# Two attention mixers in a decoder trunk: attention steps at set places between the products, weights split four pieces ahead, rotary on GpSimd

## The chip, the cores and the metric

The kernel runs on one NeuronCore of a Trainium2 chip. The metric is the device time of one launch in microseconds (us). Its engines are named as the profile names them: PE (TensorE matmul), PEld (TensorE weight load), DVE (VectorE), ACT (ScalarE), POOL (GpSimd), SP (SyncE, which issues the DMAs here).

## What is computed

The reference is a two-layer decoder trunk on 256 tokens of width 1024, all in float32. Each layer is a SwiGLU half-step, an attention mixer with 16 heads of 64, and a second SwiGLU half-step (inner width 2816). Cut to what matters here:

```python
def mixer_a(h, w_qkv, w_o, pos):
    qkv = (h @ w_qkv).reshape(B, S, 3, N_HEADS, HEAD_DIM).transpose(2, 0, 3, 1, 4)
    q, k, v = partial_rotary(qkv[0], pos), partial_rotary(qkv[1], pos), qkv[2]
    ...
    return o.transpose(0, 2, 1, 3).reshape(B, S, ATTN_DIM) @ w_o

def mixer_b(h, w_q, w_o, k_pad, v_pad, k_mean, pos):
    q = partial_rotary((h @ w_q)..., pos)
    ...
    return out @ w_o

for layer in range(2):
    h = h + 0.5 * swiglu(rmsnorm(h, ffn1_norm[layer]), ...)
    hn = rmsnorm(h, mix_norm[layer])
    h = h + (mixer_a(hn, ...) if layer == 0 else mixer_b(hn, ...))
    h = h + 0.5 * swiglu(rmsnorm(h, ffn2_norm[layer]), ...)
    if layer == 0:
        shared = shared_kv(h, kv_norm, kv_w, pos)
return rmsnorm(h, final_norm)
```

Mixer a mixes three dilated causal patterns; with 256 tokens they come down to one softmax with a mask that counts in how many patterns a key occurs. Mixer b takes k and v from `shared_kv` and, with one block of 256, is plain causal attention. So both mixers are the same program with other inputs: projections of q, k and v, rotary on 16 of the 64 columns of q and k, masked softmax, values, and an output projection.

## The kernel before

**Exact products.** A float32 operand is split into a high part (rounded by ScalarE, L151 for weights, L89 for others) and the rest (a subtraction on VectorE, L152, L91, L93), and each product is three matmuls: high by high, high by low, low by high (`product`, L177). A piece of weights is 128 partitions by 1024 values; a unit is one raw buffer of 1 MB, mostly two pieces (`unit`, L137; `pieces_of`, L144). There are four raw buffers and eight buffers each for high and low parts.

**The mixer** (`mixer`, L533) works through four groups of four heads. For one group `projections` (L552) forms k and v together, 512 columns wide, 8 blocks of the inner dimension by 2 halves of the tokens, then q, 256 wide; each product is one step of a generator, which yields its estimated cost. ScalarE takes the sums out with the norm's scale (L567, L582), `rotate` (L446) turns 16 columns of each head in four VectorE instructions (L453 to L456), and `turn_in` (L542) transposes q and k on TensorE (L549) and splits them.

**Attention** (`attend`, L458) goes by pairs of heads, eight pairs in all. `scores` (L466): 12 small matmuls (L473) into two PSUM tiles, mask and row minimum on VectorE (L481), exponentials on ScalarE (L484), reciprocal (L486), and the normalisation by four GpSimd instructions (L489). `turn` (L491): three transposes of one head's probabilities (L494) and their split. `values` (L499): four matmuls a head (L508, L510) into one PSUM tile for both heads, brought together by ScalarE and VectorE (L511, L512), and split into a block for the output projection. `out_t` (L409) multiplies the eight blocks; five of them as they come, the last three at the end, one output tile after the other.

**What sets the order.** `weave` (L274) runs two generators side by side, the attention and the feed (projections of the later groups, then output projection), and takes the next step from the one that is behind by its share of the estimated cost (20.4 against 59.0). `START` = 50 steps of the feed go first. A group's attention may begin when `finished` (L585) has marked the group ready. The kernel is written in a framework whose planner then sets each engine's order and the waits: the order of the text counts as priority, and an instruction that the planner takes to be ready may go ahead of an earlier one that it takes to be waiting. On the chip each engine goes through its own list in order.

PSUM is eight banks: five accumulators and three tiles for scores and transposes (`accp`, `trp`).

## Time and profile before

| | us |
|---|---|
| median of 3 runs (lowest, highest) | 1023.26 (1021.39, 1024.11) |
| the profiled execution | 1023.26 |
| its span, first to last instruction | 1021.5 |
| busy: PE / DVE / ACT / POOL | 994.7 / 724.6 / 592.0 / 178.1 |
| mean granted TensorE clock | 0.993 |

The span is what the trace covers; the execution's own time lies 1.8 us above it. Busy time is the time in which an engine had an instruction running. Since matmuls are pipelined and their ends are modelled, a matmul's own duration overlaps the next one's; the distance between starts is what a product costs in a stream. A row of waits names the instruction that stood waiting, what ended the wait, the total, the number of times and the longest. The granted clock is the share of full speed that TensorE was given.

### The profile page before, as it was taken

The page shows a single profiled execution, that of the slowest core. Times are in us where ns is not written, and L with a number is a line of the kernel's source. Part 1 is how long each engine was busy: PE and PEld are TensorE (multiplying, and loading weights), DVE is VectorE, ACT ScalarE, POOL GpSimd, SP SyncE. Part 2 cuts the span into 40 slices and gives each one's busy share as a digit, 9 for nine tenths or more (in the row PEclk, how much of TensorE's full clock was granted, in tenths as well). Part 3 has the DMA queues.
Part 4 walks back from the last instruction along what each step waited for, and adds up shares of the span by engine and source line. Part 5 has one row for each costly group of instructions (what it writes and reads, how often), then busy time and mean ns, then how long its engine had stood idle before and what let it go on. Part 6 is the DMA issues. An engine that isn't in the chain of part 4 may idle for free.

```text
span 1021.5 us, 15730 instructions
## 1 busy us (share of the span) xinstructions
PE 994.7 (97%) x5899; PEld 871.0 (85%) x5899; DVE 724.6 (71%) x1252; ACT 592.0 (58%) x1092; POOL 178.1 (17%) x211
## 2 busy tenths in 40 slices
PE   8999999999899999999999999999999999999997
PEld 6888888887798888888888888888878888888886
DVE  7978865666676788876678878665667678878642
ACT  6766564456666566565456665444666565665531
POOL 3111101203224211110112111010222222111000
PEclk9999999999999999999999999999999999999999
DMA  9885556653331565666655664666333444655611
GB/s 306 254 261 166 195 190 201 198 174 115 124 125 61 184 209 170 191 196 187 206 164 178 198 201 148 224 206 202 129 124 104 144 124 141 207 189 180 207 67 42
DMA packets 158428, 176.05 MB, mean 172 GB/s; under 512 B 3600, under 2 KB 152336, under 8 KB 158352
## 3 DMA queue, kind: packets, MB, share of 16 engines
q1 hardware_dynamic: 157920, 174.50, 53.6%
q8 instruction: 46, 0.75, 0.3%
q10 hardware_dynamic: 432, 0.55, 0.2%
q14 instruction: 30, 0.25, 0.1%
HBM read 173.99 MB, written 1.05 MB: 171 GB/s over the span
## 4 chain that ended last, share of the span: by engine, by line
PE 88%; ACT 6%; DVE 3%; POOL 1%; issue 1%; DMA 0%; POOLq 0%; ACTq 0%; DVEq 0%
PE f_u L191 16%; PE f_g L191 15%; PE dn_f L191 12%; PE f_u L194 8%; PE f_g L194 8%; PE dn_f L194 6%; PE dn_f_d L182 2%; PE dn_f_d L180 2%; PE dn_f_d L184 2%; PE kv_b L184 1%; PE kv_b L182 1%; PE kv_b L180 1%; PE kv_a L184 1%; PE kv_a L180 1%; PE kv_a L182 1%
## 5 line engine op out<-in xcount | busy, mean ns | idle before, releaser
L191 PE MATMUL f_g<-x_n,wh_f_g 128*128 128x512 f32 x688 | 180.1, 394 | 0.0
L191 PE MATMUL f_u<-x_n,wh_f_u 128*128 128x512 f32 x688 | 177.7, 391 | 2.3 <-DVE j_f_g L309 2.3
L191 PEld LDWEIGHTS f_u<-x_n,wh_f_u 128*128 128x128 f32 x688 | 128.8, 188 | 30.2 <-issue 2.1
L191 PEld LDWEIGHTS f_g<-x_n,wh_f_g 128*128 128x128 f32 x688 | 124.0, 189 | 22.6
L327 POOL TENSOR_TENSOR j_f_u<-j_f_u,r_n 128x256 f32<-128x256 f32 x88 | 76.0, 865 | 383.0 <-DVE j_f_u L309 363.8
L191 PE MATMUL dn_f<-act_f,wh_f 128*128 128x512 f32 x528 | 126.5, 391 | 0.0
L152 DVE TENSOR_TENSOR wl_f_u<-raw_f_u,wh_f_u 128x1024 fp32r<-128x1024 f32 x86 | 119.6, 1392 | 1.8 <-ACT wh_f_u L151 1.7
L152 DVE TENSOR_TENSOR wl_f_g<-raw_f_g,wh_f_g 128x1024 fp32r<-128x1024 f32 x86 | 104.5, 1244 | 22.6 <-PE f_g L194 14.4
L191 PEld LDWEIGHTS dn_f<-act_f,wh_f 128*128 128x128 f32 x528 | 96.8, 188 | 18.6
L152 DVE TENSOR_TENSOR wl_f<-raw_f,wh_f 128x1024 fp32r<-128x1024 f32 x72 | 81.8, 1153 | 36.1 <-ACT wh_f L151 26.8
L194 PE MATMUL f_g<-x_n,wl_f_g 128*128 128x256 f32 x688 | 103.4, 282 | 0.0
L194 PE MATMUL f_u<-x_n,wl_f_u 128*128 128x256 f32 x688 | 103.4, 283 | 0.0
L194 PEld LDWEIGHTS f_g<-x_n,wl_f_g 128*128 128x128 f32 x688 | 96.8, 190 | 6.5
L151 ACT ACTIVATE wh_f_g<-raw_f_g 128x1024 fp32r<-128x1024 f32 x86 | 89.5, 1049 | 16.3 <-issue 6.0
L151 ACT ACTIVATE wh_f<-raw_f 128x1024 fp32r<-128x1024 f32 x72 | 67.3, 978 | 49.5 <-PE dn_f L191 27.2
L151 ACT ACTIVATE wh_f_u<-raw_f_u 128x1024 fp32r<-128x1024 f32 x86 | 86.7, 1047 | 15.0 <-PE f_g L191 10.9
L194 PEld LDWEIGHTS f_u<-x_n,wl_f_u 128*128 128x128 f32 x688 | 91.7, 192 | 0.5 <-DVE wl_f_u L152 0.4
L228 POOL TENSOR_TENSOR ss_n<-ss_n,sq_n 128x256 f32<-128x256 f32 x42 | 43.0, 1024 | 200.7 <-ACT sq_n L227 197.1
L89 ACT ACTIVATE act_f<-j_f_g 128x256 fp32r<-128x256 f32 x88 | 36.4, 417 | 71.0 <-DVE j_f_g L328 70.8
L325 ACT ACTIVATE j_f_g<-j_f_g 128x256 f32<-128x256 f32 x88 | 36.8, 418 | 63.2 <-DVE j_f_g L324 62.7
L194 PEld LDWEIGHTS dn_f<-act_f,wl_f 128*128 128x128 f32 x528 | 68.1, 191 | 2.8
L194 PE MATMUL dn_f<-act_f,wl_f 128*128 128x256 f32 x528 | 69.0, 283 | 0.0
(193 smaller groups left out, 1820.0 us busy)
## 6 DMA issues: line engine op xcount, KB each, us to landing
raw_f_g<-in_ffn_w_gate_dram SPq DMA_DIRECT2D x43, 1024.0 KB, 5.3
raw_f_u<-in_ffn_w_up_dram SPq DMA_DIRECT2D x43, 1024.0 KB, 5.3
raw_f<-in_ffn_w_down_dram SPq DMA_DIRECT2D x24, 1024.0 KB, 5.2
raw_f_d<-in_ffn_w_down_dram SPq DMA_DIRECT2D x11, 1024.0 KB, 5.0
raw_f<-in_ffn_w_down_dram SPq DMA_DIRECT2D x12, 768.0 KB, 4.4
raw_kva<-in_a_w_qkv_dram SPq DMA_DIRECT2D x16, 512.0 KB, 4.3
raw_kvb<-in_kv_w_dram SPq DMA_DIRECT2D x16, 512.0 KB, 4.4
raw_qa<-in_a_w_qkv_dram SPq DMA_DIRECT2D x4, 1024.0 KB, 5.2
```

Of the source, the lines that this page charges most:

```text
L89: nc.scalar.activation(hi, src, AF.Copy, scale=scale)
L151: nc.scalar.activation(wh, r, AF.Copy)
L152: nc.vector.tensor_sub(wl, r, wh.bitcast(F32))
L180: nc.tensor.matmul(ac, xh, wh, start=first, stop=False)
L182: nc.tensor.matmul(ac, xh, wl, start=False, stop=False)
L184: nc.tensor.matmul(ac, xl, wh, start=False, stop=last)
L191: nc.tensor.matmul(ac, wh, flat(x), start=first and i == 0, stop=False)
L194: nc.tensor.matmul(ac[:, :S], wl, x[:, 0, :], start=False, stop=last and i == len(ws) - 1)
L228: nc.gpsimd.tensor_tensor(self.ss, self.ss, sq, op=ALU.add)
L325: nc.scalar.activation(g, g, AF.Silu)
L327: nc.gpsimd.tensor_tensor(u, u, norm.row, op=ALU.mult)
```

## The change

An `Agenda` replaces `weave`. It counts the estimated time of the product steps, and every attention step is put on it with a distance from the moment that releases it: a group's two pairs get eight fixed distances after the group's second `turn_in`, other ones for the last group; `turn_in` comes 3.6 after the evacuation that completes q and k. `Pieces` holds the weights of the whole mixer as one list: asking for a piece first splits all up to four pieces further on, and loads raw units two ahead of the split. In mixer a, q and k are projected together (512 wide) and v after them (256 wide); in mixer b, k and v together and then q, but in the last group k, q and v one by one. `rotate` goes from VectorE to GpSimd. `attend` becomes `attention`, which hands out its three steps; `out_t` takes its weights from the list. The feed-forward parts are untouched. In the diff, parts that only go away are cut.

```diff
--- before.py
+++ after.py
@@ -26,8 +26,7 @@
 NG = H // HG
 ROT = 16
 HALF = ROT // 2
-EXTRA = 1
-START = 50
+LEAD = 4
 EPS = 1e-6
 SCALE = DH ** -0.5
 BIG = 1e30
@@ -250,41 +249,54 @@
             return by_token(self.x)
 
 
-
...
+    class Agenda:
+        def __init__(self):
+            self.now, self.calls = 0.0, []
+
+        def after(self, wait, call, *args):
+            self.calls.append((self.now + wait, call, args))
+            self.calls.sort(key=lambda c: c[0])
+
+        def run_next(self):
+            _, call, args = self.calls.pop(0)
+            call(*args)
+
+        def run(self, steps):
+
+            for cost in steps:
+                if cost is None:
+                    self.run_next()
                     continue
...
+                self.now += cost
+                while self.calls and self.calls[0][0] <= self.now:
+                    self.run_next()
+
+    class Pieces:
+
+
+
+        def __init__(self, specs):
+            self.specs, self.raws, self.parts = specs, [], []
+
+        def load(self, u):
+            while len(self.raws) <= min(u, len(self.specs) - 1):
+                name, k, n, srcs = self.specs[len(self.raws)]
+                raw = rawp.tile([P, k, n], F32, tag="raw", name=f"raw_{name}")
+                for dst, src in srcs:
+                    nc.sync.dma_start(raw if dst is None else raw[:, :, dst], src)
+                self.raws.append(raw)
+
+        def split(self, i):
+            while len(self.parts) <= min(i, 2 * len(self.specs) - 1):
+                u, j = divmod(len(self.parts), 2)
+                self.load(u + 2)
+                name, k, n, _ = self.specs[u]
+                k //= 2
+                self.parts.append(pieces_of(f"{name}_{j}", self.raws[u][:, j * k:j * k + k], k, n))
+
+        def __getitem__(self, i):
+            self.split(i + LEAD)
+            return self.parts[i]
 
 
     def down_t(name, w, blocks, norm):
@@ -406,10 +418,9 @@
                 part(t, slice(c * 512 + o, c * 512 + o + n))
             after(t)
 
-    def out_t(name, w, blocks, norm, tail=4 - EXTRA):
+    def out_t(name, pieces, base, blocks, norm, tail=3):
 
         accs = [acc(f"ot_{name}_{i}") for i in range(KD // 2)]
-        held = []
 
         def step(i, k, ws):
             wh, wl = ws
@@ -421,17 +432,16 @@
                 nc.tensor.matmul(ac, wh[:, d], lo, start=False, stop=False)
                 nc.tensor.matmul(ac, wl[:, d], hi, start=False, stop=k == KD - 1 and j == 1)
 
...
+        for k in range(KD - tail):
+            ws = pieces[base + k][0]
+            while len(blocks) <= k:
+                yield None
+            for i in range(KD // 2):
+                step(i, k, ws)
+                yield 0.72
+        held = [(k, pieces[base + k][0]) for k in range(KD - tail, KD)]
+        while len(blocks) < KD:
+            yield None
         for i in range(KD // 2):
             for k, ws in held:
                 step(i, k, ws)
@@ -450,18 +460,18 @@
         sn = rot[:, t, 1:2, :].to_broadcast([P, n, ROT])
         ta = sp.tile([P, n, ROT], F32, tag="rota", name=f"ra_{name}", bufs=2)
         tb = sp.tile([P, n, ROT], F32, tag="rotb", name=f"rb_{name}", bufs=2)
-        nc.vector.tensor_mul(ta, v[:, :, :ROT], cs)
-        nc.vector.tensor_mul(tb[:, :, :HALF], v[:, :, HALF:ROT], sn[:, :, :HALF])
-        nc.vector.tensor_mul(tb[:, :, HALF:], v[:, :, :HALF], sn[:, :, HALF:])
-        nc.vector.tensor_add(v[:, :, :ROT], ta, tb)
-
-    def attend(operands, mask, name, blocks):
+        nc.gpsimd.tensor_tensor(ta, v[:, :, :ROT], cs, op=ALU.mult)
+        nc.gpsimd.tensor_tensor(tb[:, :, :HALF], v[:, :, HALF:ROT], sn[:, :, :HALF], op=ALU.mult)
+        nc.gpsimd.tensor_tensor(tb[:, :, HALF:], v[:, :, :HALF], sn[:, :, HALF:], op=ALU.mult)
+        nc.gpsimd.tensor_tensor(v[:, :, :ROT], ta, tb, op=ALU.add)
+
+    def attention(operands, mask, name, blocks):
 
 
 
         segs = [slice(t * P, t * P + (t + 1) * P) for t in range(NT)]
         owns = [slice(i * DH, (i + 1) * DH) for i in range(2)]
-        sms = {}
+        sms, pTs = {}, {}
 
         def scores(p):
             g, b = divmod(p, HG // 2)
@@ -494,14 +504,15 @@
                 nc.tensor.transpose(tr[:, n * P:(n + 1) * P], sms[p, i][:, n * P:(n + 1) * P], ident)
             pT = pp.tile([P, 2, 3 * P], F32R, tag="pT", name=f"pT_{name}{p}_{i}")
             parts_of(pT[:, 0], pT[:, 1], tr)
-            return pT
-
-        def values(p, pTs):
+            pTs[p, i] = pT
+
+        def values(p):
             g, b = divmod(p, HG // 2)
             po = acc(f"po_{name}{p}")
             s = etile(f"o_{name}{p}")
             vs = operands(g)[1]
-            for i, (own, pT) in enumerate(zip(owns, pTs)):
+            for i, own in enumerate(owns):
+                pT = pTs[p, i]
                 v0, v1 = [flat(v[:, 2 * b + i]) for v in vs]
                 ac = po[:, i * S:(i + 1) * S]
                 for n in range(2):
@@ -513,98 +524,94 @@
             x = atile([P, 2, S], F32R, name=f"oT_{name}{p}")
             parts_of(x[:, 0], x[:, 1], s)
             blocks.append(x)
-
...
-        table(AF.Silu, blocks[-1][:, 0, 0:1].bitcast(F32))
-
-    def mixer(name, normkv, xkv, wk, wv, normq, xq, wq, wo, mask, after):
+            if len(blocks) == KD:
+                table(AF.Silu, x[:, 0, 0:1].bitcast(F32))
+
+        return scores, turn, values
+
+    def mixer(name, segs, wo, mask, after):
+
 
 
         n = HG * DH
-        blocks, ready, turns, qks, vss = [], set(), {}, {}, {}
-
-        def operands(g):
-            return (qks[g], vss[g]) if g in ready else None
+        blocks, turns, qks, vss = [], {}, {}, {}
+        specs = []
+        for g in range(NG):
+            for norm, x, parts in segs(g):
+                k = 2048 // (n * len(parts))
+                for k0 in range(0, KD, k):
+                    specs.append((f"{''.join(p[0] for p in parts)}{name}{g}_{k0}", k, n * len(parts),
+                                  [(slice(i * n, i * n + n), rows(w, k0, k, c0 + g * n, n))
+                                   for i, (_, w, c0) in enumerate(parts)]))
+        base = 2 * len(specs)
+        specs += [(f"{name}o_{u}", 2, D, [(None, rows(wo, 2 * u, 2, 0, D))]) for u in range(KD // 2)]
+        pieces = Pieces(specs)
+        agenda = Agenda()
+        scores, turn, values = attention(lambda g: (qks[g], vss[g]), mask, name, blocks)
 
         def turn_in(g, t):
 
             if t == 0:
                 qks[g] = [ap_.tile([P, 4, NT, P], F32R, tag=f"qk{i}", name=f"qk{i}_{name}{g}", bufs=2) for i in "hl"]
-            s = turns.pop((g, t)).rearrange("p a b -> p (a b)")
+            s = turns[g, t].rearrange("p a b -> p (a b)")
             tr = trt(f"qt_{name}{g}_{t}")
             for k in range(4):
                 nc.tensor.transpose(tr[:, k * P:(k + 1) * P], s[:, k * P:(k + 1) * P], ident)
             parts_of(*[x[:, :, t, :] for x in qks[g]], tr.rearrange("p (k n) -> p k n", n=P))
-
...
+            if t == NT - 1:
+                p = 2 * g
+                for wait, call, args in ((3.0, scores, (p,)), (8.5, scores, (p + 1,)), (11.0, turn, (p, 0)),
+                                         (12.3, turn, (p, 1)), (15.0, values, (p,)), (17.0, turn, (p + 1, 0)),
+                                         (18.2, turn, (p + 1, 1)), (20.7, values, (p + 1,))) if g < NG - 1 else (
+                                         (3.0, scores, (p,)), (5.0, scores, (p + 1,)), (9.5, turn, (p, 0)),
+                                         (10.3, turn, (p, 1)), (11.2, turn, (p + 1, 0)), (12.0, turn, (p + 1, 1)),
+                                         (12.4, values, (p,)), (14.0, values, (p + 1,))):
+                    agenda.after(wait, call, *args)
+
+        def evacuate(g, t, r, ac, parts, missing):
+            for m, (kind, _, _) in enumerate(parts):
+                src = ac[:, m * n:(m + 1) * n]
+                if kind == "v":
+                    v = atile([P, HG, 2, DH], F32R, name=f"vs_{name}{g}_{t}")
+                    vss.setdefault(g, []).append(v)
+                    parts_of(v[:, :, 0], v[:, :, 1], src.rearrange("p (j d) -> p j d", d=DH), r)
+                    continue
+                if (g, t) not in turns:
+                    turns[g, t] = atile([P, 2 * HG, DH], name=f"rt_{name}{g}_{t}")
+                slots = slice(0, HG) if kind == "q" else slice(HG, 2 * HG)
+                nc.scalar.activation(flat(turns[g, t][:, slots]), src, AF.Copy, scale=r)
+                missing.discard(kind)
+                if not missing:
+                    rotate(turns[g, t], t, f"{name}{g}_{t}")
+                    agenda.after(3.6, turn_in, g, t)
+
+        def projections():
+            i = 0
+            for g in range(NG):
+                missing = [{"q", "k"} for t in range(NT)]
+                for norm, x, parts in segs(g):
+                    wide = n * len(parts)
+                    label = "".join(p[0] for p in parts)
+                    if wide == 512:
+                        acs = [acc(f"{label}_{name}{g}_{t}") for t in range(NT)]
+                    else:
+                        ac = acc(f"{label}_{name}{g}")
+                        acs = [ac[:, t * n:(t + 1) * n] for t in range(NT)]
+                    k = 1024 // wide
+                    for k0 in range(0, KD, 2 * k):
+                        for t in range(NT):
+                            for kk in range(k0, k0 + 2 * k):
+                                w = pieces[i + (kk - k0) // k][kk % k]
+                                product([acs[t]], *x[t][kk], [w], kk == 0, kk == KD - 1)
+                                yield 0.68 if wide == 512 else 0.36
+                            if norm.col is None and (t == NT - 1 or k0 + 2 * k == KD):
+                                norm.finish()
+                            if k0 + 2 * k == KD:
+                                evacuate(g, t, norm.col[t], acs[t], parts, missing[t])
+                        i += 2
+
+        agenda.run(projections())
+        agenda.run(out_t(f"{name}o", pieces, base, blocks, after))
 
 
     def first(k):
@@ -622,12 +629,21 @@
     late_constants()
     xs = n1.xs()
     w = a["a_w_qkv"][0]
-    mixer("a", n1, xs, (w, H * DH), (w, 2 * H * DH), n1, xs, (w, 0), a["a_w_o"][0], masks[:, 0, :], n2)
+    mixer("a", lambda g: [(n1, xs, [("q", w, 0), ("k", w, H * DH)]), (n1, xs, [("v", w, 2 * H * DH)])],
+          a["a_w_o"][0], masks[:, 0, :], n2)
     ffn("f20", 0, 2, n2, n3)
     kx = []
     ffn("f11", 1, 1, n3, n5, beside=[lambda k=k: kx.append(gain(k, 3, "kx", "kx")) for k in range(KD)])
-    w = a["kv_w"]
-    mixer("b", n3, by_token(kx), (w, 0), (w, H * DH), n5, n5.xs(), (a["b_w_q"][0], 0), a["b_w_o"][0], masks[:, 1, :], n6)
+    wq = ("q", a["b_w_q"][0], 0)
+    wk, wv = ("k", a["kv_w"], 0), ("v", a["kv_w"], H * DH)
+    xkv, xq = by_token(kx), n5.xs()
+
+    def segs_b(g):
+        if g < NG - 1:
+            return [(n3, xkv, [wk, wv]), (n5, xq, [wq])]
+        return [(n3, xkv, [wk]), (n5, xq, [wq]), (n3, xkv, [wv])]
+
+    mixer("b", segs_b, a["b_w_o"][0], masks[:, 1, :], n6)
     blocks = ffn_blocks("f21", a["ffn2_w_gate"][1], a["ffn2_w_up"][1], n6)
 
     h = [[xp.tile([P, 512], F32, tag=f"kx{2 * t + c}", name=f"h_{t}_{c}") for c in range(2)] for t in range(NT)]
```

More of the change, by code (lines that the diff above doesn't have):

```diff
@@ L585, in finished @@
-        def finished(g, steps):
-            for i, cost in enumerate(steps):
-                yield cost
-                if i == 4:
-                    turn_in(g, 1)
-                    yield 0.45
-                if i == 8:
-                    ready.add(g)
-        wsteps = out_t(f"{name}o", wo, blocks, after)
-        def feed():
-            yield from projections(0)
-            for g in range(1, NG):
-                yield from finished(g - 1, projections(g))
-            yield from finished(NG - 1, some(wsteps, 16))
```

88 lines of the change are left out of this document (removed).

## The prediction

> **What bounds the kernel now.** I read the page first, then busy time by stretch, then TensorE's waits. The page:
>
> ```profile
> PE 994.7 (97%) x5899; PEld 871.0 (85%) x5899; DVE 724.6 (71%) x1252; ACT 592.0 (58%) x1092; POOL 178.1 (17%) x211
> ```
>
> TensorE is busy for 97% of the span, so the change can pay only where TensorE now stands still or runs slow. The change touches the two mixers alone. By the timeline mixer a runs from 194.55 us (its first k/v product) to 325.72 (first product of the next feed-forward) and mixer b from 696.89 to 827.75. The windows of these two stretches (PE, PEld, DVE, ACT, POOL busy, clock, DMA share, GB/s):
>
> ```profile
> 194.55:325.72 131.17, 123.15 (x822) 107.65 (x821) 87.22 (x208) 81.69 (x183) 30.97 (x38) 0.97 0.40 128
> 696.89:827.75 130.86, 122.74 (x822) 107.49 (x821) 87.29 (x208) 81.78 (x183) 29.99 (x38) 0.97 0.40 128
> ```
>
> Two nearly equal stretches of 131 us, each with 8 us of idle TensorE and a mean granted clock of 0.97. The view of waits names the idle time (total us, times, longest):
>
> ```profile
> PE pt_a L494 <- POOL sm_a L489: 3.7, 5, 1.2
> PE pt_b L494 <- POOL sm_b L489: 3.6, 5, 1.2
> ...
> PE po_b L508 <- ACT pT_b L89: 2.2, 1, 2.2
> PE po_a L508 <- ACT pT_a L89: 2.2, 1, 2.2
> ...
> PE po_b L508 <- DVE o_b L512: 1.2, 2, 0.8
> PE po_a L508 <- DVE o_a L512: 1.2, 2, 0.8
> PE q_b L180 <- ACT rt_b L582: 0.8, 2, 0.5
> ```
>
> And the clock, by slices of 10 us of mixer a:
>
> ```profile
> 230.00:240.00 10.00, 8.66 (x49) 7.89 (x50) 5.64 (x21) 6.32 (x16) 6.08 (x8) 0.83 0.18 75
> 310.00:320.00 10.00, 9.38 (x64) 9.18 (x65) 4.31 (x8) 4.06 (x8) 1.19 (x2) 0.83 0.32 105
> ```
>
> A slice at 0.83 loses 10 x 0.17 = 1.7 us. There are two in mixer a, and mixer b's mean of 0.97 says the same two there. Both follow the waits of the probability transposes (L494), at the first pair of heads and at the last:
>
> ```profile
> 224.76 0.33 PE L473 MATMUL s_a<-qkh_a 64*128 64x128 f32 x2
> ...
> 230.75 0.33 PE L494 MATMUL pt_a<-ident,sm_a 128*128 128x128 f32 x1 [1.08 <-POOL sm_a L489]
> ```
>
> So the bound is TensorE, with a loss in each mixer where an attention step comes up before the chain scores, exponentials, GpSimd normalisation, transposes is through.
>
> **The change part by part.** All sums are made against the profiled execution: 1023.26 us, its span 1021.5 and 1.8 us around it. It is also the median of the runs shown, so no correction is needed.
>
> *Attention steps at set places.* The agenda counts product time as it is, by the chain that ended last, where 16 products of 512 columns follow 16 of 256:
>
> ```profile
> 148.77 3.65 PE dn_f L191 x16
> 152.42 1.91 PE dn_f L194 x16
> ```
>
> 3.65/16 = 0.228 us a wide product and 1.91/16 = 0.120 a narrow one; three a step, 0.68 and 0.36, as in the agenda. How long does the chain need? In the first pair above, from scores at 224.76 to the first transpose at 230.75: 6.0 us. The second head's part is ready when GpSimd is through with the pair, and that is paced by
>
> ```profile
> 227.48 0.28 DVE L481 CUSTOM_DVE_ANT_0 sm_a<-s_a,masks 128x128 f32<-128x128 f32 x1
> 230.07 6.08 POOL L489 TENSOR_SCALAR sm_a<-sm_a,ls_a 128x128 f32<-128x128 f32 x8 [26.94 <-DVE nm_a L481]
> ```
>
> that is 6.08/2 = 3.0 us a pair, so 230.07 + 3.0 - 224.76 = 8.3 us. This chain already carries a delay (VectorE starts on it only 2.7 us after the scores). The new table puts the transposes 8.0 and 9.3 us of products after a pair's scores, and TensorE's own attention steps between (two scores of six row pairs like the first above, some 0.15 us a pair, 0.9 each: an estimate) add 1.8: 9.8 and 11.1 against 6.0 and 8.3. For the first three groups the L494 waits should go. In the last group the table is tighter: the first pair's transposes come 6.5 + 1.8 = 8.3 and 7.3 + 2.1 = 9.4 after its scores (0.3 for a head's three transposes, estimated from the single one above), spare 2.3 and 1.1. The second pair's normalisation queues behind the first's on GpSimd, done at 8.3 + 1.5 = 9.8 and 8.3 + 3.0 = 11.3, and its transposes come at 8.2 + 2.4 = 10.6 and 9.0 + 2.7 = 11.7: spare 0.8 and 0.4. Before, this group's transposes followed the scores with less between them and waited. I take all 3.7 + 3.6 = **7.3 us** back, and with them the slow clock, 4 x 1.7 = **6.8 us**. The bounds: nothing back of the tail's share (half of both, 7.1), or all.
>
> The wait for the copied probabilities (po on ACT pT, 2.2 in each mixer) stood where ScalarE had exponentials and evacuations to do first. The table leaves 2.7 us between a second transpose and its values; the copies (ScalarE, then the second part on VectorE) take 0.48 + 0.55, and one split in front makes 2.1:
>
> ```profile
> L89 ACT ACTIVATE pT_a<-pt_a 128x384 fp32r<-128x384 f32 x16 | 7.6, 481 | 1.0 <-PE pt_a L494 1.0
> L151 ACT ACTIVATE wh_qa<-raw_qa 128x1024 fp32r<-128x1024 f32 x6 | 6.4, 1060 | 2.3 <-PE kv_a L184 1.8 <-ACT vs_a L89 0.5
> ...
> L582 ACT ACTIVATE rt_a<-q_a,c_n 128x256 f32<-128x256 f32 x8 | 3.8, 472 | 1.1 <-PE q_a L184 1.1
> ```
>
> I take back **4.4**; bounds 0 and 4.4. The 1.2 + 1.2 on o_a and o_b stay: `values` still writes both heads into one PSUM tile, the second after the first is read. The 0.8 on rt_b stays too: two token halves share one accumulator, and the second waits until the first is evacuated.
>
> *Projections.* In mixer a the work is regrouped, not changed (512 columns wide for q and k, 256 for v). But now v has the shared accumulator, and its evacuation takes ScalarE and then VectorE, 0.47 and about as much again, where q's took 0.47; if one step of another product (0.68) fills in, as now at q, 0.3 is open in each of four groups: **+1.1**, bounds 0 and 4 x 0.95 = 3.8. In the last group of mixer b, k and v part into 256-wide products: 48 x (2 x 0.120 - 0.228) = **+0.5 us**. q and k first lets the last group's attention begin while v (5.8 us) still runs, so that v's 16 x 0.36 and the output projection's 20 x 0.72, 20.2 us in all, cover the 3.6 + 14.0 = 17.6 us up to the last `values`.
>
> *Splits four ahead.* The same 6 pieces a group pass ScalarE (1.06 each) and VectorE, and the same 1 MB units come through SP into the same four raw buffers, with the DMA engines 40% busy in the mixers (rows above). TensorE waits for neither a split nor a transfer there now, so nothing is gained. Asked for earlier, a split can stand in front of an attention step; the chain's 2.7 us are already such a delay. What I charge is the end of mixer b, where the table packs four `values`, six transposes and two scores into 11 us of products and some 7 us of attention steps on TensorE:
>
> ```profile
> L152 DVE TENSOR_TENSOR wl_ao<-raw_ao,wh_ao 128x1024 fp32r<-128x1024 f32 x8 | 9.7, 1222 | 3.5 <-ACT wh_ao L151 3.5
> L91 DVE TENSOR_TENSOR pT_a<-pt_a,pT_a 128x384 fp32r<-128x384 f32 x16 | 8.8, 554 | 1.3 <-ACT pT_a L89 0.8
> ...
> L481 DVE CUSTOM_DVE_ANT_0 sm_a<-s_a,masks 128x256 f32<-128x256 f32 x16 | 6.7, 419 | 0.0
> L512 DVE TENSOR_TENSOR o_a<-po_a,o_a 64x256 f32<-64x256 f32 x16 | 6.6, 413 | 7.7 <-ACT o_a L511 7.7
> ...
> L456 DVE TENSOR_TENSOR rt_a<-ra_a,rb_a 128x128 f32<-128x128 f32 x8 | 2.3, 292 | 0.2
> L453 DVE TENSOR_TENSOR ra_a<-rt_a,rot 128x128 f32<-128x128 f32 x8 | 2.3, 282 | 0.4 <-ACT rt_a L582 0.3
> L454 DVE TENSOR_TENSOR rb_a<-rt_a,rot 128x64 f32<-128x64 f32 x8 | 2.0, 249 | 0.0
> L455 DVE TENSOR_TENSOR rb_a<-rt_a,rot 128x64 f32<-128x64 f32 x8 | 1.7, 213 | 0.0
> ```
>
> VectorE there has 4 splits, 6 copies pT, 4 masked scores of 256 and 4 of 128 (0.28), and 8 sums o: 4.9 + 3.3 + 1.7 + 1.1 + 3.3 = 14.3 of 18 us, the smaller ones left out. I charge one split, **+1.2**; bounds 0 and 4.9 (all four).
>
> *Rotary on GpSimd.* VectorE gives up the last four of these rows, 0.28 + 0.25 + 0.21 + 0.29 = 1.04 us, 16 times: 16.6 us that lay beside TensorE's work. GpSimd's price for these shapes is not in the trace. Its nearest two-input rows:
>
> ```profile
> L327 POOL TENSOR_TENSOR j_f_u<-j_f_u,r_n 128x256 f32<-128x256 f32 x88 | 76.0, 865 | 383.0 <-DVE j_f_u L309 363.8 <-DVE r_n L247 19.2
> ...
> L661 POOL TENSOR_TENSOR var<-var,ssq 128x1 f32<-128x1 f32 x1 | 0.2, 189 | 1.1 <-ACT sq L651 1.1
> ```
>
> The line through them gives 0.53 at 128 elements and 0.36 at 64, so 2 x 0.53 + 2 x 0.36 = 1.8 us; the ends are 4 x 0.19 = 0.8 and 4 x 0.87 = 3.5. I take 1.8. With two evacuations at 0.47 the path to `turn_in` is 2.7 us against the 3.6 set aside: no wait, where GpSimd is free. Where a pair's normalisation (3.0) stands in front, it is 5.7, a wait of up to 2.1, and behind the waiting `turn_in` transposes stand, on TensorE, all the products that follow. That can meet the 12 turns of the later groups, since from the second group on a pair is always under way; I let half of them wait 0.4 us: **+2.4**, bounds 0 and 12 x 2.1 = 25.
>
> The Trainium skill, "GPSIMD Engine Reference", section "When to use GPSIMD", speaks against this edit: elementwise work belongs on VectorE, GpSimd being about twice as slow with two inputs. By it the rotary would take 2 x 1.04 = 2.1 us, an estimate, still inside the 3.6, and the sum would not move; no run so far shows these shapes on GpSimd.
>
> Sum: 7.3 + 6.8 + 4.4 - 1.1 - 0.5 - 1.2 - 2.4 = 13.3 us, **1010 us**.
>
> **The rivals.**
> - *The tail still waits.* Spare times of 0.8 and 0.4 us are small. Besides, the last group turns all four heads before its first `values`, with two buffers for the copies: the second pair's copies can't start before the first pair's products, at 12.4 by the table, and two copies of 1.0 then stand between those and the `values` at 14.0. If the last pairs wait as now, half of the transposes' waits and of the slow clock stay, 7.1: 1017.
> - *The slow clock has another cause.* Then 6.8 us stay: 1017. For: one wait of 2.2 us (po on pT) brought no slow slice. Against: both slow slices follow L494 waits, in either mixer. The Trainium skill's "TensorE: Matmul & The Clock Gate", section "Why this matters for your kernels", would have it so, naming idle gaps above about 3 us as what brings half clock; the trace has half-clock stretches after shorter ones, and I follow the trace.
> - *The placing is not kept.* A k/v product of the next group stands between the q products of the first, which the text puts ahead of it all:
>
> ```profile
> 209.35 0.28 PE L184 MATMUL q_a<-wh_qa,x_n 128*128 128x256 f32 x1
> 209.47 0.40 PE L180 MATMUL kv_a<-wh_kva,x_n 128*128 128x512 f32 x1
> ```
>
> So the order on TensorE is not the text's alone. If the planner moves the steps back to where they wait, 7.3 + 6.8 stay: 1024, no change that can be told.
> - *GpSimd becomes the bound, slower than before.* Rotary and normalisation in one queue; each of the 12 turns waits 2.1 us (25 in all), the idle time keeps the slow clock (6.8 not won): 1023.3 - 7.3 - 4.4 + 1.1 + 0.5 + 1.2 + 25 = 1039. It turns slower than before where the mean wait at the turns is above (11.7 - 2.8)/12 = 0.7 us. For: GpSimd is in order, and a pair's 3.0 us falls near the evacuations. Against: GpSimd is busy 31 of 131 us in a mixer, and would be 31 + 8 x 1.8 = 45.
>
> **How the numbers follow.** The forecast 0.57, the tail 0.14, the clock 0.04, the placing 0.10, GpSimd 0.15. A measurement of this kernel tells about 0.3%, 3 us, from no change. Faster: 0.57 + 0.14 + 0.04 = 0.75; same: 0.10; slower: 0.15. The range begins where every mixer wait goes and no new one comes, 1023.3 - 18.5 - 2.4 - 0.8 + 0.5 = 1002, less the restarts: a matmul after a wait lasts 0.33 us (the one at 230.75) where one in the stream comes every 0.12, so 0.1 to 0.2 us for each of the 18 waits in the rows above, 2 to 3 us, 999; it ends above the placing's 1024, at 1026, and leaves out GpSimd's case.
>
> **What would show it.** Right: both mixers some 124 to 125 us long instead of 131; no slice of theirs below clock 1; no row for pt on POOL sm; VectorE near 708 us busy, GpSimd near 207. Wrong: a row of qt waiting for POOL rt with several us (GpSimd's case); pt on POOL sm at the last pair (the tail); wl or wh rows among TensorE's waits (splits too late); rotary rows on GpSimd far above 0.53 and 0.36 us.

## The result, and the profile after

| | before | after |
|---|---|---|
| median, us (lowest, highest) | 1022.85 (1021.39, 1024.11) | 1037.91 (1036.90, 1043.38) |
| the profiled execution / its span, us | 1023.26 / 1021.5 | 1037.39 / 1035.3 |
| mixer a / mixer b, us | 131.17 / 130.86 | 141.69 / 134.17 |
| mean granted TensorE clock | 0.993 | 0.987 |

The changed kernel is slower: ratio 1.0159, 95% interval 1.0120 to 1.0197. The forecast was 1010, the range 999 to 1026. The span grew by 13.8 us and the two mixers by 10.5 + 3.3 = 13.8, so the feed-forward parts have no share in it.

The page of the changed kernel first:

```profile
PE 996.0 (96%) x5947; PEld 875.6 (85%) x5947; DVE 714.4 (69%) x1188; ACT 592.7 (57%) x1092; POOL 221.9 (21%) x275
```

TensorE is still the engine that counts. GpSimd went from 178.1 to 221.9 us, 15 more than the 207 that the prediction named, and at 21% it does not look like a bound. The waits of TensorE say otherwise (what waited, for whom: us in total, times, longest):

```profile
PE qt_a L559 <- POOL rt_a L466: 10.2, 4, 3.4
PE qt_b L559 <- POOL rt_b L466: 7.7, 3, 3.0
PE q_b L179 <- ACT rt_b L582: 2.8, 4, 1.6
PE f_u L190 <- DVE j_f_g L321: 2.3, 4, 0.9
PE po_b L519 <- DVE o_b L523: 2.2, 2, 1.9
PE v_a L179 <- DVE vs_a L92: 2.1, 3, 0.8
PE po_a L519 <- DVE o_a L523: 1.9, 4, 1.1
```

The rows of pt on sm (7.3 us) and of po on pT (4.4) are gone, as forecast. In their place stand 17.9 us in which the transposes of q and k (`turn_in`) wait for the rotary on GpSimd. Nearly all of it falls on six instructions, the first `turn_in` of each later group, in either mixer: 3.21, 3.35 and 3.44 us in a, 3.01, 2.99 and 1.68 in b. One of them, on GpSimd's timeline (start, duration, line, operation):

```profile
219.74 4.61 POOL L499 TENSOR_SCALAR sm_a<-sm_a,ls_a 128x128 f32<-128x128 f32 x4 [9.49 <-DVE ls_a L496]
225.47 3.94 POOL L499 TENSOR_SCALAR sm_a<-sm_a,ls_a 128x128 f32<-128x128 f32 x4 [1.11 <-DVE ls_a L496]
229.38 0.45 POOL L463 TENSOR_TENSOR ra_a<-rt_a,rot 128x128 f32<-128x128 f32 x1
229.79 1.30 POOL L464 TENSOR_TENSOR rb_a<-rt_a,rot 128x64 f32<-128x64 f32 x1
231.05 0.32 POOL L465 TENSOR_TENSOR rb_a<-rt_a,rot 128x64 f32<-128x64 f32 x1
231.44 0.45 POOL L466 TENSOR_TENSOR rt_a<-ra_a,rb_a 128x128 f32<-128x128 f32 x1
```

and on ScalarE's, TensorE's and VectorE's:

```profile
224.99 0.81 ACT L582 ACTIVATE rt_a<-qk_a,c_n 128x256 f32<-128x256 f32 x2
```

```profile
231.95 1.11 PE L559 MATMUL qt_a<-ident,rt_a 128*128 128x128 f32 x4 [3.21 <-POOL rt_a L466]
```

```profile
229.59 1.32 DVE L151 TENSOR_TENSOR wl_va<-raw_va,wh_va 128x1024 fp32r<-128x1024 f32 x1 [0.62 <-ACT wh_va L150]
```

Read together: q and k are copied out by 225.80. GpSimd took up the normalisation of the group's second pair at 225.47, 0.33 us earlier, and is held by it until 229.4. Only then come the four rotary instructions. One of them takes 1.30 us where its twin takes 0.32; it began while VectorE's split ran (229.59 to 230.91) and ended 0.18 us after it. TensorE wanted the tile at 231.95 - 3.21 = 228.74.

In mixer b the share of the two is another. At its first long wait (TensorE wanted the tile at 747.92) ScalarE's copy and GpSimd's instructions are

```profile
743.82 0.45 ACT L582 ACTIVATE rt_b<-q_b,c_n 128x256 f32<-128x256 f32 x1
```

```profile
744.29 2.99 POOL L499 TENSOR_SCALAR sm_b<-sm_b,ls_b 128x128 f32<-128x128 f32 x4 [1.78 <-DVE ls_b L496]
747.25 1.48 POOL L463 TENSOR_TENSOR ra_b<-rt_b,rot 128x128 f32<-128x128 f32 x1
```

The copy is through at 744.27, the normalisation goes first all the same, from 744.29, and the rotary behind it takes 3.6 us where 1.54 is usual: two of its four instructions are held up.

The granted clock, in the two mixers and in the window around mixer a's first long wait (PE, PEld, DVE, ACT, POOL busy, clock, DMA share, GB/s):

```profile
194.64:336.33 141.69, 126.93 (x822) 112.33 (x821) 82.37 (x176) 81.80 (x184) 53.13 (x70) 0.93 0.35 118
707.51:841.68 134.17, 121.19 (x871) 108.84 (x870) 81.79 (x176) 81.83 (x185) 51.94 (x70) 0.99 0.37 125
230.00:240.00 10.00, 8.05 (x43) 7.80 (x43) 3.42 (x6) 3.01 (x7) 3.24 (x7) 0.66 0.29 105
```

A clock of 0.66 over 10 us is 6.8 us at half clock. The clock's records show three such stretches in mixer a, from 230.82, 261.54 and 292.26 us, and one of 3.4 us in b, from 814.50. The first and the last as windows:

```profile
230.82:237.65 6.83, 5.70 (x27) 5.70 (x28) 1.20 (x3) 0.98 (x2) 2.42 (x7) 0.50 0.42 154
814.50:817.91 3.41, 3.41 (x18) 3.41 (x17) 2.17 (x11) 2.43 (x9) 1.37 (x2) 0.50 0.02 5
```

Each of the three begins inside a long wait, 1.1 to 1.4 us before it ends, and idle time at half clock costs nothing extra: 3.8 of their 20.5 us fall into the waits. The one in b follows no wait of qt but one of 1.92 us of po on o. So the clock takes (20.5 - 3.8 + 3.4)/2 = 10.1 us, where before it took 6.7, counted the same way.

The account against the kernel before, by the windows (length less PE busy): idle time in the two mixers went from 8.0 + 8.1 to 14.8 + 13.0 us, 11.6 more, and the clock takes 3.4 more: 15.0 together, where 13.8 are measured. Against the forecast: qt waits 17.9 in place of 2.4 are 15.5, clock 10.1 in place of 0: 1010 + 15.5 + 10.1 = 1035.6, 1.8 short of the profiled execution, since smaller terms were off too (below).

### The profile page after: what moved, and what is told of

Same layout as the page of the kernel before. It is cut to its first block, busy times and chain, and to the rows that moved or that the text cites. A ratio compares the mean times of both kernels' runs of the same rounds, so it can differ in the third digit from the quotient of the medians.

```text
span 1035.3 us, 15836 instructions
## 1 busy us (share of the span) xinstructions
PE 996.0 (96%) x5947; PEld 875.6 (85%) x5947; DVE 714.4 (69%) x1188; ACT 592.7 (57%) x1092; POOL 221.9 (21%) x275
```

## The experiments

**Theory.** Normalisation and rotary share GpSimd's queue, and the new table makes the one stand in front of the other in every later group; TensorE's wait then lowers its clock. **Rivals:** the rotary is too slow on GpSimd wherever it stands; GpSimd's instructions are held up by VectorE's splits; the loss comes from elsewhere in the new order (the splits four ahead, the projections' order). Medians below are in us, ratios are against the kernel before on the same chip (1022 to 1023 each time).

**1. Rotary back on VectorE** (the changed kernel otherwise).

```diff
-        nc.gpsimd.tensor_tensor(ta, v[:, :, :ROT], cs, op=ALU.mult)
+        nc.vector.tensor_mul(ta, v[:, :, :ROT], cs)
...
```

> The changed kernel with the rotary back on VectorE, all else as changed. Theory (queue): the rotary stood on GpSimd behind a pair's normalisation, TensorE waited 17.9 us for it at the first q/k transposes of the groups and ran 11.9 us' worth at half clock after that; both go, 1037.9 - 29.8 = 1008 us, no row for qt on POOL. Rival (table): 3.6 us after the evacuation is too early whoever does the rotary; qt then waits for DVE rt, 1025 us or more.

1013.29, ratio 0.9906 (0.9891 to 0.9921). The qt row has gone. Its mixers are 123.77 and 128.90 us:

```profile
194.47:318.24 123.77, 119.48 (x823) 104.76 (x822) 87.10 (x208) 81.55 (x184) 37.98 (x38) 1.00 0.41 135
689.42:818.32 128.90, 122.82 (x870) 110.04 (x869) 87.42 (x208) 81.58 (x184) 33.30 (x38) 0.97 0.40 130
```

So the whole loss hangs on that edit, and the rest of the change is worth about 9.7 us, somewhat less than the 15 expected. A half-clock stretch of 6.8 us is left in mixer b.

**2. The kernel before with the rotary on GpSimd**, the same four lines the other way.

> The kernel before with the rotary on GpSimd and nothing else changed. Theory (queue): where an evacuation falls into a pair's normalisation the q/k transposes wait; by the trace of before that is clearly so at one turn in each mixer (normalisation 230.07 to 236.15, transposes at 236.68), 1 to 2 us of wait each and perhaps a half-clock stretch: 1025 to 1030 us. Rival (placing): GpSimd is harmless and the new order of steps cost the time: 1023 us within 2.

1023.48, ratio 1.0009 (0.9995 to 1.0023): nothing. The 1025 to 1030 that I expected was wrong, and the rival's 1023 came. In the old order the same edit brings qt waits of 1.6 us in all. The edit is not dear by itself, but with the new order.

**3. Normalisation on VectorE, rotary left on GpSimd.**

```diff
-                    nc.gpsimd.tensor_scalar(sms[p, i][:, seg], sms[p, i][:, seg], ls[:, i, t:t + 1], None, op0=ALU.mult)
+                    nc.vector.tensor_scalar_mul(sms[p, i][:, seg], sms[p, i][:, seg], ls[:, i, t:t + 1])
```

> The changed kernel with the rotary on GpSimd as changed, but the normalisation of the probabilities on VectorE, so that nothing stands ahead of the rotary on GpSimd. Theory (queue): the waits for POOL rt go, 1008 to 1014 us, the upper end if VectorE's added four instructions a pair are felt. Rival (speed): GpSimd's rotary is too slow for the 3.6 us set aside, being blocked by VectorE's splits (1.3 us where 0.3 to 0.45 is usual); then qt still waits 0.5 to 1.5 us at most groups, 1018 us or more.

1011.64, ratio 0.9893 (0.9877 to 0.9910). With the queue to itself the rotary on GpSimd costs nothing: the qt waits are 0.5 us in all, and the clock is full in both mixers:

```profile
194.49:318.56 124.07, 119.58 (x822) 104.88 (x821) 88.42 (x208) 81.60 (x184) 24.06 (x38) 1.00 0.42 135
689.73:815.89 126.16, 120.21 (x870) 107.39 (x869) 89.48 (x208) 81.28 (x184) 21.79 (x38) 1.00 0.40 132
```

Either job alone on GpSimd is harmless; both in one queue, in this order, are not.

**4. Idle matmuls in the waits.** The changed kernel with work that has no use in front of the first `turn_in` of the later groups; their sums are overwritten.

```diff
+            if g and t == 0:
+                for i in range(14):
+                    nc.tensor.matmul(tr, fill[:, :P], fill, start=True, stop=True)
             for k in range(4):
```

> The changed kernel with 14 idle bf16 matmuls of 512 columns (about 3.1 us, results overwritten) ahead of the first q/k transposes of the later groups, where TensorE waits now. It computes the same. Theory (the half clock follows from TensorE's idling): the waits for POOL rt turn into these matmuls, no half-clock stretch follows, 11.9 us less, about 1.5 us more at the last group of mixer b whose wait was shorter: 1027 to 1029 us. Rival (the clock has another cause): half-clock stretches stay, 1038 to 1041 us.

1030.26, ratio 1.0072 (1.0057 to 1.0087): 7.7 us better than the changed kernel though no useful work comes earlier. It lies 1.3 us above the band. One half-clock stretch of 3.4 us is left in the mixers, and the 7.7 us are near the 8.4 that mixer a's three stretches cost outside the waits. So the clock's share is a consequence of the idle time, and a wait here is paid more than once: its own length, and part of what follows at half speed.

**5. Second pair's scores earlier**, at 5.0 in place of 8.5.

```diff
-                for wait, call, args in ((3.0, scores, (p,)), (8.5, scores, (p + 1,)), (11.0, turn, (p, 0)),
+                for wait, call, args in ((3.0, scores, (p,)), (5.0, scores, (p + 1,)), (11.0, turn, (p, 0)),
```

> The changed kernel with one number changed: the second pair's scores of the first three groups at 5.0 instead of 8.5 (the rotary stays on GpSimd, and every engine keeps its work). Theory (queue): the second pair's normalisation is through some 3.5 us earlier and the rotary meets a free GpSimd; the six waits of about 3 us and the half clock behind them go, 1009 to 1014 us. Rival (speed: GpSimd's rotary is late by itself): the waits stay, 1035 us or more.

1028.94, ratio 1.0075 (1.0056 to 1.0094): a miss by 15 us. The 3.2 us wait became 2.5, the qt waits 11.0 in all, and half clock 10.2 us in place of 23.9. GpSimd's timeline in this kernel, at the same place:

```profile
219.65 9.11 POOL L499 TENSOR_SCALAR sm_a<-sm_a,ls_a 128x128 f32<-128x128 f32 x8 [9.50 <-DVE nm_a L491]
228.73 0.45 POOL L463 TENSOR_TENSOR ra_a<-rt_a,rot 128x128 f32<-128x128 f32 x1
```

The two pairs' normalisations now stand back to back and take 9.11 us, 1.14 each, not the 6.08 for eight that the trace of before showed. GpSimd loses only its 1.11 us of idle time and is free 0.65 us sooner. Here it is its throughput that binds, not only the order of its queue. I had priced its instructions from an undisturbed stretch.

**6. VectorE's weight splits cut in four.** The changed kernel with each of the mixers' subtractions of 1024 columns made four of 256.

```diff
-            nc.vector.tensor_sub(wl, r, wh.bitcast(F32))
+            c = kk * n // cuts
+            for i in range(cuts):
+                nc.vector.tensor_sub(flat(wl)[:, i * c:i * c + c], flat(r)[:, i * c:i * c + c],
+                                     flat(wh)[:, i * c:i * c + c].bitcast(F32))
```

> The changed kernel with VectorE's part of each mixer split (1.22 us in one instruction) cut in four instructions of 256 columns; nothing else. Theory (port: a GpSimd instruction that meets a running two-input VectorE instruction waits for its end): GpSimd's slow instructions of 1.3 to 1.7 us become 0.8 to 1.1 us, the waits for POOL rt shrink by 1 to 2 us each, 1022 to 1032 us. Rival (GpSimd's slow instructions have another cause): their times stay, 1037 to 1041 us with VectorE's added 0.4 us a split.

1026.19, ratio 1.0040 (1.0020 to 1.0059). GpSimd's rows of this kernel (line, shapes, count, busy us, mean ns, idle before),

```profile
L502 POOL TENSOR_SCALAR sm_a<-sm_a,ls_a 128x128 f32<-128x128 f32 x16 | 11.7, 733 | 65.1 <-DVE ls_a L499 61.6 <-PE pt_a L507 3.5
L466 POOL TENSOR_TENSOR ra_b<-rt_b,rot 128x128 f32<-128x128 f32 x8 | 4.7, 593 | 2.7 <-ACT rt_b L585 2.7
L469 POOL TENSOR_TENSOR rt_a<-ra_a,rb_a 128x128 f32<-128x128 f32 x8 | 3.8, 481 | 0.6
```

against those of the changed kernel:

```profile
L499 POOL TENSOR_SCALAR sm_a<-sm_a,ls_a 128x128 f32<-128x128 f32 x16 | 15.8, 991 | 65.1 <-DVE ls_a L496 65.1
L463 POOL TENSOR_TENSOR ra_b<-rt_b,rot 128x128 f32<-128x128 f32 x8 | 7.1, 892 | 2.7 <-ACT rt_b L582 2.7
L466 POOL TENSOR_TENSOR rt_a<-ra_a,rb_a 128x128 f32<-128x128 f32 x8 | 5.4, 676 | 0.6
```

Same instructions, same data; the edit shortens VectorE's alone. In the changed kernel's trace 26 of GpSimd's 128 instructions for rotary and normalisation last over 0.25 us more than the quickest of their shape, 23.6 us more in all. 25 of the 26 began while VectorE ran a split, the other 0.02 us before one. With the splits cut it is 13 instructions and 5.7 us. The qt waits fell from 17.9 to 11.8 us. So the hold-up is real and worth a third of the waits; the queue holds the rest.

The Trainium skill, "SBUF — State Buffer", section "SBUF: two separate sides", says that VectorE with two SBUF inputs and GpSimd contend for one pair of ports, that whoever starts first keeps it for the whole instruction, and that the other stands still until then. The 25 of 26 and the 1.30 us row that ended just behind the split agree with it. The hold-up goes the other way too: five instructions that began within a split weren't held; one met its last 0.09 us, and the other four stand beside two splits that took 2.12 and 1.53 us where 1.22 is usual.

**7. No split lead** (kernel 1 with `LEAD = 0`).

> The changed kernel with the rotary on VectorE (as in e1_rot_dve, 1013.3 us) and weights split when their first product is asked for (LEAD 0 instead of 4). Theory: TensorE waited for no split before and the planner already fetches splits ahead where buffers are free, so the lead is worth nothing: 1013 us within 3. Rival: the lead is a main part of what the rest of the change won; waits for wh or wl appear, 1018 us or more.

1012.44, ratio 0.9909 (0.9892 to 0.9925), as kernel 1. Splitting four pieces ahead gains and costs nothing that these runs can tell.

**8. k and v ahead of q everywhere** (kernel 1 with the old order of projections).

```diff
-    mixer("a", lambda g: [(n1, xs, [("q", w, 0), ("k", w, H * DH)]), (n1, xs, [("v", w, 2 * H * DH)])],
+    mixer("a", lambda g: [(n1, xs, [("k", w, H * DH), ("v", w, 2 * H * DH)]), (n1, xs, [("q", w, 0)])],
...
-        if g < NG - 1:
+        if g < NG:
```

> The changed kernel with the rotary on VectorE (as in e1_rot_dve, 1013.3 us) and k and v projected ahead of q in all groups of both mixers, as before the change. Theory: q and k first pays at the last group alone, where v's 5.8 us of products stand behind the last turn; without it the output projection's 14.4 us must cover 17.6 us of steps, so 3 us of waits in each mixer and a half-clock stretch of 1.7 to 3.4 us: 1019 to 1026 us. Rival: the end was not short of products, 1013 us within 2.

1016.75, ratio 0.9947 (0.9932 to 0.9962): 3.5 us slower than kernel 1. I had expected 6 to 13. The last pairs of each mixer wait for their normalisation again:

```profile
PE pt_b L504 <- POOL sm_b L499: 1.7, 2, 1.3
PE pt_a L504 <- POOL sm_a L499: 1.7, 2, 1.3
```

which is what q and k first removes.

**9. The queue alone.** The changed kernel with the second pair's normalisation behind the rotary of both halves of the next group. The planner would put it in front again, so two small instructions make its factor depend on the rotated tile. TensorE's order is unchanged.

```diff
+        def normal(p, held=None):
+            ls = lss[p]
+            if held is not None:
+                z = sp.tile([P, 2 * NT], F32, tag="z", name=f"z_{name}{p}", bufs=2)
+                nc.gpsimd.tensor_scalar(z, flat(held)[:, :2 * NT], 0.0, None, op0=ALU.mult)
+                nc.gpsimd.tensor_tensor(flat(ls), flat(ls), z, op=ALU.add)
...
-                for wait, call, args in ((3.0, scores, (p,)), (8.5, scores, (p + 1,)), (11.0, turn, (p, 0)),
+                for wait, call, args in ((3.0, scores, (p,)), (8.5, scores, (p + 1,)), (13.1, lambda: normal(p + 1, turns[g + 1, NT - 1]), ()), (11.0, turn, (p, 0)),
```

> The changed kernel, with GpSimd's queue alone reordered: for the first three groups the normalisation of the second pair of heads stands behind the rotary of both token halves of the next group instead of ahead of it. Two small GpSimd instructions on 4 columns (a factor made from the rotated tile, zero, added to the reciprocal sums) hold it there; TensorE's order is that of the changed kernel, and both jobs stay on GpSimd. Theory (the wait at qt is the queue: the rotary stands behind the normalisation): in the stretch at 222 to 232 us of the changed kernel the rotary could start when rt is copied, 225.8, and end at 227.4 to 228.4, and qt was wanted at 228.7; so the qt waits on rt, 17.9 us in all, fall under 3 us, most of the 11.9 us of half clock goes, and the second pair's transposes wait up to 1 us each: 1011 to 1019. Rival (the rotary is too slow on GpSimd wherever it stands, because VectorE's splits hold it up): qt still waits over 1 us at each of the first turns, and the time stays over 1022.

1021.85, ratio 0.9991 (0.9980 to 1.0002): 16 us better than the changed kernel, but 3 above the band. On GpSimd's timeline the rotary now starts as soon as the copy is there and is through before 228.74, though it is still held up once (1.37):

```profile
225.81 0.46 POOL L463 TENSOR_TENSOR ra_a<-rt_a,rot 128x128 f32<-128x128 f32 x1 [1.54 <-ACT rt_a L592]
226.23 0.33 POOL L464 TENSOR_TENSOR rb_a<-rt_a,rot 128x64 f32<-128x64 f32 x1
226.51 0.33 POOL L465 TENSOR_TENSOR rb_a<-rt_a,rot 128x64 f32<-128x64 f32 x1
226.91 1.37 POOL L466 TENSOR_TENSOR rt_a<-ra_a,rb_a 128x128 f32<-128x128 f32 x1
```

and TensorE's waits are

```profile
PE pt_a L514 <- POOL sm_a L509: 5.0, 9, 0.7
...
PE qt_b L569 <- POOL rt_b L466: 2.0, 2, 1.7
PE po_a L529 <- DVE o_a L533: 1.9, 4, 1.1
PE pt_b L514 <- POOL sm_b L509: 1.8, 3, 0.7
```

The qt waits went from 17.9 to about 2 by the order of one queue, with the hold-ups nearly unchanged (24 instructions, 21.8 us). But the normalisation is late now, and 6.8 us of waits stand at pt. In neither order did the one queue serve both in time: the order decides who waits.

**10 to 12. Towards a better version.** From kernel 3: both heads' products ahead of either evacuation in `values` (10), and with it an accumulator for each token half where the products are 256 wide (11); then the same two edits on kernel 9, with both jobs on GpSimd (12).

```diff
                     nc.tensor.matmul(ac[:, P:], v1, pT[:, n, S:], start=False, stop=n == 1)
+            for i, own in enumerate(owns):
+                ac = po[:, i * S:(i + 1) * S]
                 nc.scalar.activation(s[own], ac[DH:], AF.Copy)
...
-                        ac = acc(f"{label}_{name}{g}")
-                        acs = [ac[:, t * n:(t + 1) * n] for t in range(NT)]
+                        acs = [acc(f"{label}_{name}{g}_{t}")[:, :n] for t in range(NT)]
```

> The kernel with the normalisation on VectorE, and in values the products of both heads ahead of either head's evacuation, so that the second head's products do not wait until the first half of the shared accumulator is read. Theory (the po waits, 1.9 + 0.9 us there, come from the two heads' shared accumulator): both rows of po on o go, 1008 to 1010, against 1011.6 for the kernel that it is made from. Rival: the next user of the accumulator or of oT waits instead, and the time is the same, 1011 to 1013.

> The same kernel, and beside that an accumulator of its own for each token half where the products are 256 columns wide (v in mixer a, k, q and v in mixer b). Theory (the waits of v on vs, 1.8, and of q on rt, 2.7 us, come from the shared accumulator): they go too, and the time falls by about 4 us more, to 1004 to 1006. Rival: the five accumulators are then all in use, the next product waits for a free one, and the time is that of the kernel before it or longer, 1008 to 1013.

> The changed kernel with all three: second pair's normalisation queued behind the rotary on GpSimd, both heads' products ahead of the evacuations, own accumulators for the token halves. Rotary and normalisation both stay on GpSimd. If GpSimd is no bound once its queue stands in the right order, this gives the same as the kernel with the normalisation on VectorE and the same two edits, within 3 us: 1004 to 1009. If GpSimd's hold-ups by VectorE's splits still delay the transposes, it is 5 us or more slower than that kernel.

Kernel 10: 1006.68, ratio 0.9845 (0.9832 to 0.9858), 5 us for one moved loop and more than I expected. Kernel 11: **999.56**, ratio 0.9775 (0.9763 to 0.9788), better than both kernels of the study and than I expected. Kernel 12: 1005.81, ratio 0.9836 (0.9823 to 0.9849), 6.2 slower than 11. Kernel 11's waits have no row of a projection that waits for its accumulator, and po on o is down to 0.2 us in each mixer; the longest waits in the mixers are

```profile
PE qt_a L561 <- POOL rt_a L466: 2.1, 2, 1.0
...
PE pt_b L504 <- DVE nm_b L491: 1.2, 1, 1.2
```

and kernel 12's are

```profile
PE qt_b L571 <- POOL rt_b L466: 3.9, 2, 3.2
...
PE pt_a L514 <- POOL sm_a L509: 1.6, 3, 0.8
```

The 3.2 us stands at the last group of mixer b, where another pair's normalisation comes in front of the rotary and two of its instructions are held up (1.30 and 1.35 us). So with both jobs GpSimd stays a bound here, by some 6 us, even in a better order; 3.4 of these are two stretches of half clock that kernel 11 doesn't have; on VectorE, busy 728.4 of 997.7 us in kernel 11, the normalisation costs nothing that shows.

## Why the prediction was wrong

*Transposes on the normalisation, 7.3: right.* The row is gone in the changed kernel. Kernel 8 shows that part of it came from q and k first, by 3.4 us of these waits that return.

*Probability copies, 4.4: right.* No row of po on pT is left.

*Slow clock, 6.8: the cause right, the gain not had.* The clock follows TensorE's idle time (kernel 4, kernel 3), and the new waits brought more half clock than the old ones. The Trainium skill, "TensorE: Matmul & The Clock Gate", section "Why this matters for your kernels", has idle gaps above about 3 us as the cause. The traces agree in part: the three waits of 3.2 to 3.4 us in mixer a brought it and those of 3.01 and 2.99 in b did not, but kernel 1 had a stretch of 6.8 us with a wait of 1.92, and the same wait in kernel 7 brought none.

The kept traces settle more of this. In every trace the stretches begin a whole number of times 3.413 us after one another, and those in the mixers last one or two such lengths. Cut the time at full clock of all the traces, from 20 us to the end of TensorE's work, into these lengths: each of the ten in which TensorE idles 1.87 us or more is followed by half clock, none with less than 1.13 is, and in between both occur. Of mixer a's three long waits 2.0 to 2.1 us fall into one length. Those of b are each cut by an edge, 3.01 into 1.73 + 1.28 and 2.99 into 1.85 + 1.14; kernel 1's 1.92 is 1.33 + 0.59, and kernel 7's 0.93 + 0.99. So the traces fit the idle time within one such length better than the length of one wait. No edit tests this, and what decides between 1.13 and 1.87 stays open.

*v's shared accumulator, 1.1: right in place, small in size.* 2.1 in the changed kernel. Kernel 11 takes it away.

*k, v and q one by one in mixer b's last group, 0.5: too small.* In kernel 3, without slow clock, mixer b is 126.16 - 124.07 = 2.1 us longer than a. A term that I left at its old size belongs here: q on rt is 2.7 to 2.8 us, not 0.8. And the po waits on o, 2.4 before, are 4.6 in kernel 1. Kernel 1 missed the forecast without its rotary term by 1013.29 - 1007.6 = 5.7 us. These two terms, 1.9 and 2.2 us, and 3.1 us lost to the half clock left in its mixer b are 7.2; the 1.2 charged for a split, which didn't fall due, takes most of the excess.

*Splits four ahead, nothing: right* (kernel 7). *One split at mixer b's end, 1.2: the wrong engine.* The 1.92 us of po on o in kernel 1 end when ScalarE evacuates o, at 787.32, behind the four exponentials of the next pair (785.43 to 787.30).

*Rotary on GpSimd, +2.4: this is the step that failed.* The prediction says: "I let half of them wait 0.4 us". A row of qt waiting for GpSimd's rt with several us is what it named as a sign of being wrong. Measured are 17.9 us, six waits of 1.7 to 3.4 and hardly any at the second halves. Three things were wrong in it.
- The wait was not a matter of chance, and the code gives it. A group of mixer a is 16 x 0.68 + 16 x 0.36 = 16.64 on the agenda. Its first half of q and k is complete at 12 x 0.68 = 8.16 and its second `turn_in` comes at 10.88 + 3.6 = 14.48. So the next group's first rotary is released 16.64 + 8.16 - 14.48 = 10.3 after that `turn_in`, and the second pair's scores stand at 8.5, every time. For mixer b's second and third group the same count gives 10.2. With the scores' own 0.9 us between, the normalisation starts 3.8 us after they do (221.72, by the timeline of TensorE, to 225.47) and the copies are through 4.1 after (225.80). The normalisation then keeps the queue for 3.94. The 0.33 us don't decide it: the planner lays down the order of GpSimd's list, and at the two waits of 3.0 us in mixer b the normalisation also goes first, with the copy through 0.02 us before it starts.
- The price of a pair's normalisation, 3.0, came from a quiet stretch. Beside the splits it was 3.94 and 4.61, and a rotary of 1.54 took 2.5 in mixer a and 2.8 to 3.6 in b.
- The clock was left out. The prediction let it recover on the ground that the old waits go, in the same sum that added new ones.

*The rival "GpSimd becomes the bound", 1039: this is what happened.* Its price was near by luck in part: 25 us of waits (measured 17.9) and 6.8 of clock not won (measured 10.1 lost) are 7.1 too much and 3.3 too little, 1035 together, and the smaller terms make up the rest. What spoke against it, GpSimd's 31 of 131 us, was an average over the mixer. It says nothing on whether the queue is free when the rotary is released. Its chance of 0.15 was too small by that.

## What to carry to other kernels

When a step moves to another engine, don't weigh its load but its queue: write down what is queued there at the time when the step is released, and in a hand-written schedule work this out from the distances, since it then happens in every round. Take the prices on GpSimd from a stretch in which VectorE is as busy as it will be. And after such a wait is gone, look for accumulators shared by two halves: two edits of that kind were worth 12 us here, more than the whole change without its rotary.

## What was not expected of the hardware

- A GpSimd instruction of 0.32 to 0.45 us took up to 1.48 when it began beside a VectorE split, and ended 0.18 to 0.33 us after it.
- A wait costs TensorE somewhat more than its length. From kernel 10 to kernel 11 mixer a became 122.21 - 119.60 = 2.6 us shorter, while its idle time by the trace went only from 2.79 to 2.68. By the distances between matmul starts, 2.6 us are gone at v's products, of which the named waits were 1.4. Each of the three waits of 0.47 us stands as 0.80 between two starts where 0.12 is usual, so 2.0 in all; what takes the rest was not tried.
- Half clock came in lengths of 3.41 or 6.83 us, on one grid through the whole execution, and the two waits of 3.0 us that an edge of the grid cut brought none.
